# Modulation chunks spread 3, 2, 2, 2, 3, 2, 2, 0 beside the eight gate pairs instead of two beside each

## The chip, the cores and the metric

The kernel runs on one core of a Trainium2 chip. The metric is the time of one execution on the device in microseconds (us). The names of the engines are those of the profile: PE is TensorE (PEld its weight loads), DVE is VectorE, ACT is ScalarE, POOL is GpSimd, and SP issues DMA transfers.

## The reference, cut to what matters

One layer of a hybrid encoder works on 1056 tokens (1024 of a prompt, 32 of a sample) with a model width of 1024. What bears on the change is this:

```python
mod = (jax.nn.silu(c) @ w_ada + b_ada).reshape(B, 6, 1, D_MODEL)
shift1, scale1, gate1, shift2, scale2, gate2 = [mod[:, i] for i in range(6)]
h = _rms_norm(x, norm1_g) * (1 + scale1) + shift1
proj = h @ w_in
q, k, v, xin, gb, gc, ga_br, gb_br = jnp.split(proj, IN_SPLITS, axis=-1)
...
m = jax.nn.sigmoid(ga_br) * y_a + jax.nn.sigmoid(gb_br) * y_b
x = x + gate1 * (m @ w_out)
h2 = _rms_norm(x, norm2_g) * (1 + scale2) + shift2
```

The modulation `mod` is a product of two vectors (one for the prompt, one for the sample) with a 1024 x 6144 matrix. Its parts shift1 and scale1 are needed first of all; gate1, scale2, shift2 and gate2 only behind the attention. Everything is float32.

## The kernel before, in words

Each float32 operand is split into a high and a low part (`split`: an ACT cast, L84, and a subtraction, L85, on DVE as a rule), and a product is three matmuls. The projections of the convolution and of the gates are computed transposed, two blocks of 128 columns at a time, by Strassen's scheme with seven products (`strassen`, L166 to L199): k = 0 to 6 are seven groups of 2 x 12 matmuls (L181), each half of the group 264 columns wide. Behind k = 0 ACT copies a product (L185), behind k = 1 and 2 DVE adds (L188, L191), behind k = 4, 5 and 6 DVE adds the results (L197), and ACT takes the sigmoids (L553); SP stores the gates (L555). `wstrassen` loads (L107) and prepares the weights of a pair.

The stage of the change is the loop over the two gate sections and four pairs of blocks each (L541 to L561): eight gate pairs. Behind the matmuls of each pair stand calls of `ada_step`. Such a step opens one chunk of the modulation and closes an older one. A chunk is 128 of the 6144 columns. To open it (`ada_dve`, L345 to L370) SP loads 512 KB of w_ada (L351, two buffers `adw`), and DVE forms the products along the 1024 rows in an accumulator `adacc`, of which there are also two buffers: 2 instructions L354 and 14 L357, 16 in all. To close it, PE transposes the accumulator's two halves into a PSUM tile `pad` (L364), DVE sums them (L366), adds the bias (L367) and for the section of scale2 forms the gain (L377). A step closes the oldest chunk when more than one is open, and behind the loop the last one is closed (L562). The chunks of this stage are called c0 to c15 here, in the order in which they are opened; chunk c(n) uses the accumulator buffer of c(n-2).

Behind the loop the normalised input is loaded again, block by block, as operand `hA` of the attention's projections (`load_split`, L203 to L207: a DMA L204, a cast L84, a subtraction L85) through a stage tile `st` with two buffers, and then its last 32 columns as `hS` (L577). The first four units of these projections (L731, L732, L733; 24 matmuls each) are issued together, block by block of hA, so 96 matmuls follow hA as it comes. Each unit has a PSUM bank; a fifth unit takes the bank that the first gives back when ACT has read it (L843, L848, L853, L856, the copy of V last). Before these reads a cast of another weight, `wf` (L1033), stands on ACT, whose load (L107) goes through the same stage tile behind hS.

PE's instructions stand in the order in which the code issues them. The instructions of DVE, ACT, POOL and SP are put in order by the framework's scheduler.

Of the kernel before, what the change touches and what calls it, by code (L numbers as in the profile page):

```python
# [38 lines left out]
def hybrid_layer(tc, x_prompt, x_sample, cache_k, cache_v, state_conv, c_prompt, c_sample,  # L39
# [96 lines left out]
    def wstrassen(srcs):  # L136

        raw = [kt_stage(src) for src in srcs]
        A11, A12, A21, A22 = raw[0][:, :4], raw[0][:, 4:], raw[1][:, :4], raw[1][:, 4:]
        w = {}  # L140

        def parts(o, src, eng=None):
            w[o] = ws_tile()
            split(src, w[o][:, 0], w[o][:, 1], eng)

        parts("A11", A11)
        dve.tensor_sub(A11, A11, A21)
        S3 = A11
        dve.tensor_add(A21, A21, A22)
        S1 = A21  # L150
        parts("A22", A22)
        dve.tensor_sub(A22, A22, S3)
        S2 = A22
        parts("S2", S2)
        parts("S1", S1)
        parts("A12", A12)
        dve.tensor_sub(A12, A12, S2)
        S4 = A12
        parts("S3", S3)
        parts("S4", S4, pool)  # L160
        return w
# [4 lines left out]
    def strassen(w, gs, dest, epi, hook=None):  # L166


        st = {g: {} for g in gs}
        for k, (wo_, to_, dst) in enumerate(SEQ):  # L170
            for g in gs:
                q = st[g]
                first = dst not in q
                if first:
                    q[dst] = u_tile()[:, :QW]
                t = Top[to_, g]
                for j in range(4):
                    wh, wl = w[wo_][:, 0, j, :], w[wo_][:, 1, j, :]
                    for n, (l, r) in enumerate(((wh, 0), (wh, 1), (wl, 0))):

                        pe.matmul(q[dst], l, t[:, r, j, :], start=first and j == n == 0, stop=j == 3 and n == 2,  # L181
                                  skip_group_check=not first)
                if k == 0:
                    q["p1"] = tmp("p1")
                    act.copy(q["p1"], q["X"])  # L185
                elif k == 1:
                    q["u2"] = tmp("u2")
                    dve.tensor_add(q["u2"], q["Y"], q["p1"])  # L188
                elif k == 2:
                    q["w"] = tmp("w")  # L190
                    dve.tensor_add(q["w"], q["Z"], q["u2"])  # L191
                elif k == 3:
                    epi(0, 0, g, q["X"])
                else:
                    i, j, other = ((1, 1, "w"), (0, 1, "u2"), (1, 0, "u2"))[k - 4]
                    d = dest(i, j, g)
                    dve.tensor_add(d, q[dst], q[other])  # L197
                    epi(i, j, g, d)
                if hook:  # L199
                    hook(k, g)  # L200
# [8 lines left out]
    def win_pair(sec, n):  # L209
        return [win_v[:, :, (sec * KT + n + i) * P:(sec * KT + n + i + 1) * P] for i in range(2)]  # L210
# [136 lines left out]
    def ada_dve(sec, n, psp, tag, sbp):  # L347

        c = sec * KT + n
        st = sbp.tile([P, KT, P], F32, tag="adw", name="adw", bufs=2)  # L350
        sp.dma_start(st, wada_v[:, :, c * P:(c + 1) * P])  # L351
        acc = sbp.tile([P, 2, P], F32, tag="adacc", name="adacc", bufs=2)
        for s_ in range(2):
            dve.tensor_scalar(out=acc[:, s_, :], in0=st[:, 0, :], scalar1=sc[:, 8 * s_:8 * s_ + 1], scalar2=None,  # L354
                              op0=ALU.mult)
            for kt in range(1, KT):
                dve.scalar_tensor_tensor(out=acc[:, s_, :], in0=st[:, kt, :],  # L357
                                         scalar=sc[:, 8 * s_ + kt:8 * s_ + kt + 1], in1=acc[:, s_, :],
                                         op0=ALU.mult, op1=ALU.add)

        def close():
            pt = psp.tile([P, 512], F32, tag=tag, name="pad", bufs=2)
            for s_ in range(2):
                pe.transpose(pt[:, s_ * P:(s_ + 1) * P], acc[:, s_, :], ident)  # L364
            red = sbp.tile([P, 2], F32, tag="adred", name="adred", bufs=2)
            dve.tensor_reduce(out=red, in_=pt[:, :2 * P].rearrange("p (a b) -> p a b", a=2), axis=AX.X, op=ALU.add)  # L366
            dve.tensor_scalar(out=mod[:, c, :], in0=red, scalar1=vec[:, R_B + c:R_B + c + 1],  # L367
                              scalar2=None, op0=ALU.add)
            if sec == 4:
                scale_gain(a2, 4, n, R_G2)  # L370
        return close
# [80 lines left out]
    def pair_tile():  # L452
        return E.tile([P, 2, T], F32, tag="sg", name="sg", bufs=1)
# [64 lines left out]
    def load_qkv(h):  # L518
        w = q_tiles(h)
        for j in range(3):  # L520
            v = kt_stage(qkv_src(h, j))
            for r in (0, 1):
                split(v[:, 4 * r:4 * r + 4], w[r][0][:, j], w[r][1][:, j])
        return w
# [4 lines left out]
    def ada_step():  # L529
        if ada_todo:  # L530
            ada_open.append(ada_dve(*ada_todo.pop(0), PSB, "x", B))
        if len(ada_open) > 1 or (ada_open and not ada_todo):
            ada_open.pop(0)()
# [9 lines left out]
    for sec, dst in ((6, ga_d), (7, gb_d)):  # L543
        for p in range(0, KT, 2):
            w = wstrassen(win_pair(sec, p))
            sg = pair_tile()

            def dest(i, j, g):
                return sg[:, i, (g + 2 * j) * QW:(g + 2 * j + 1) * QW]

            def epi(i, j, g, src):
                d = dest(i, j, g)
                act.activation(d, src, AF.Sigmoid)  # L553
                if g == 1 and (i, j) in ((0, 1), (1, 0)):
                    sp.dma_start(dst[p + i], sg[:, i])  # L555

            if (sec, p) == (7, KT - 2):
                qkv_w.append(load_qkv(0))
            strassen(w, (0, 1), dest, epi)
            ada_step()  # L560
            ada_step()  # L561
    while ada_open:  # L562
        ada_open.pop(0)()
    B.release()
# [964 lines left out]
```

## Time and profile before

| | before |
|---|---|
| time of the runs shown (3) | 2136.35 us median, 2134.64 to 2137.19 |
| the profiled execution | 2132.99 us, span 2131.2 us |
| mean granted clock of TensorE | 0.982 |
| PE busy | 2031.0 us (95% of the span) |
| DVE busy | 1351.4 us (63%) |
| ACT busy | 847.1 us (40%) |
| gate pair 1 starts on PE at | 245.7 us |
| gate pair 8 ends on PE at | 413.9 us |

The profiled execution is 3.4 us shorter than the median of the runs. Times in a timeline are counted from the start of the span; in a row a first number is a start, a second the duration of the group, and what stands in brackets at the end is how long the engine was idle before it and what ended that. The granted clock (PEclk) is a share of full speed: 1.00 is 2.4 GHz, 0.50 is 1.2 GHz.

### The profile page before, as it was taken

How to read it: one execution, taken by the hardware profiler on the slowest of the kernel's cores; microseconds unless marked ns; L12 is line 12 of the kernel's file. 1: busy time of each engine (PE TensorE's matmuls, PEld its weight loads, DVE VectorE, ACT ScalarE, POOL GpSimd, SP SyncE). 2: the span in 40 equal slices, each digit the busy share in tenths (PEclk: the TensorE clock that was granted, in tenths of full speed). 3: DMA queues.
4: the chain of work that ended last, by engine and by line, in shares of the span. 5: the costliest groups of instructions: out<-in, count | busy, mean ns of one | idle time of the engine just before them, and what ended most of it. 6: DMA issues, size and time to landing. Idle time of an engine off the chain costs nothing. (4 is left out here: it accounts for less than half of the span.)

```text
span 2131.2 us, 37806 instructions
## 1 busy us (share of the span) xinstructions
PE 2031.0 (95%) x14339; PEld 1976.7 (93%) x14339; DVE 1351.4 (63%) x3096; ACT 847.1 (40%) x2044; POOL 364.7 (17%) x660
## 2 busy tenths in 40 slices
PE   7799999899999999999899989889999999999999
PEld 5799999899999999999899989879999999989998
DVE  4988799967766776677357974685555555432322
ACT  5522233366666666666222213463332332321210
POOL 1023100033333333333000000012112112100000
PEclk8899999999999999999999999999999999999999
DMA  8422254532211221121388625123222222552321
GB/s 251 151 84 90 71 161 135 192 89 60 68 57 56 62 59 54 50 69 48 114 258 250 198 90 170 53 68 122 71 73 89 70 80 79 172 157 65 99 69 57
DMA packets 298960, 224.42 MB, mean 105 GB/s; under 512 B 15617, under 2 KB 281498, under 8 KB 298778
## 3 DMA queue, kind: packets, MB, share of 16 engines
q1 hardware_dynamic: 298778, 222.00, 34.0%
q8 instruction: 113, 1.85, 0.4%
q14 instruction: 69, 0.57, 0.1%
HBM read 162.46 MB, written 59.49 MB: 104 GB/s over the span
## 5 line engine op out<-in xcount | busy, mean ns | idle before, releaser
L84 ACT CAST ws<-st 128x512 fp32r<-128x512 f32 x360 | 217.2, 615 | 564.4 <-PE u L181 172.9
L181 PE MATMUL u<-op,ws 128*128 128x264 f32 x3168 | 397.3, 285 | 7.8 <-ACT op L84 6.5
L181 PEld LDWEIGHTS u<-op,ws 128*128 128x128 f32 x3168 | 392.4, 189 | 8.4 <-ACT op L84 6.7
L85 DVE TENSOR_TENSOR ws<-st,ws 128x512 fp32r<-128x512 f32 (+1 forms) x322 | 222.6, 699 | 195.3 <-ACT ws L84 192.9
L181 PE MATMUL u<-T,ws 128*128 128x264 f32 x1536 | 198.5, 287 | 1.2 <-DVE sg L197 1.2
L181 PEld LDWEIGHTS u<-T,ws 128*128 128x128 f32 x1536 | 193.5, 190 | 1.8 <-DVE sg L197 1.8
L731 PE MATMUL b<-qw,hA 128*128 128x384 f32 x512 | 186.8, 365 | 2.5 <-DVE adred L366 1.2
L732 PE MATMUL b<-qw,hA 128*128 128x384 f32 x512 | 174.2, 340 | 0.6 <-DVE qw L688 0.6
L733 PE MATMUL b<-qw,hA 128*128 128x384 f32 x512 | 173.8, 339 | 0.0
L1431 PE MATMUL u<-ka,ws 128*128 128x352 f32 x480 | 156.8, 327 | 4.6 <-ACT ka L84 2.8
L1432 PE MATMUL u<-ka,ws 128*128 128x352 f32 x480 | 155.6, 324 | 2.3 <-DVE ka L85 2.3
L181 PE MATMUL u<-B,ws 128*128 128x264 f32 x1152 | 152.1, 287 | 4.6 <-ACT B L84 4.6
L1433 PE MATMUL u<-ka,ws 128*128 128x352 f32 x480 | 155.7, 324 | 0.0
L181 PEld LDWEIGHTS u<-B,ws 128*128 128x128 f32 x1152 | 145.6, 190 | 5.3 <-ACT B L84 4.9
L357 DVE SCALAR_TENSOR_TENSOR adacc<-adw,sc,adacc 128x128 f32<-128x128 f32 x448 | 132.8, 350 | 0.6
L879 ACT ACTIVATE p<-S,nmx,rs 128x128 f32<-128x128 f32 (+5 forms) x144 | 113.1, 787 | 50.1 <-DVE nmx L959 17.0
L85 POOL TENSOR_TENSOR ws<-st,ws 128x512 fp32r<-128x512 f32 x38 | 49.8, 1311 | 445.3 <-ACT ws L84 426.1
L731 PEld LDWEIGHTS b<-qw,hA 128*128 128x128 f32 x512 | 97.7, 191 | 6.4 <-issue 2.1
L732 PEld LDWEIGHTS b<-qw,hA 128*128 128x128 f32 x512 | 97.9, 191 | 1.2 <-DVE qw L688 0.9
L733 PEld LDWEIGHTS b<-qw,hA 128*128 128x128 f32 x512 | 97.2, 190 | 0.0
L1431 PEld LDWEIGHTS u<-ka,ws 128*128 128x128 f32 x480 | 90.6, 189 | 5.6 <-ACT ka L84 3.5
L1432 PEld LDWEIGHTS u<-ka,ws 128*128 128x128 f32 x480 | 90.7, 189 | 3.1 <-DVE ka L85 3.1
(277 smaller groups left out, 4379.8 us busy)
## 6 DMA issues: line engine op xcount, KB each, us to landing
adw<-in_w_ada_dram SPq DMA_DIRECT2D x48, 512.0 KB, 4.0
st<-in_w_gate_up_dram SPq DMA_DIRECT2D x44, 512.0 KB, 4.0
st<-in_w_in_dram SPq DMA_DIRECT2D x43, 512.0 KB, 4.3
sa<-a_d SPq DMA_DIRECT2D x22, 528.0 KB, 3.6
a_d<-xa SPq DMA_DIRECT2D x84, 132.0 KB, 1.7
st<-in_w_in_dram SPq DMA_DIRECT2D x42, 256.0 KB, 2.9
st<-in_w_down_dram SPq DMA_DIRECT2D x16, 512.0 KB, 5.0
h_d<-xnT SPq DMA_DIRECT2D x8, 528.0 KB, 4.3
```

What stands on the lines that cost most here:

```text
L84: act.copy(hi, src)
L85: (lo_eng or dve).tensor_sub(lo, src, f(hi))
L181: pe.matmul(q[dst], l, t[:, r, j, :], start=first and j == n == 0, stop=j == 3 and n == 2, skip_group_check=not first)
L357: dve.scalar_tensor_tensor(out=acc[:, s_, :], in0=st[:, kt, :], scalar=sc[:, 8 * s_ + kt:8 * s_ + kt + 1], in1=acc[:, s_, :], op0=ALU.mult ...
L731: pe.matmul(pj[:, 0:384], a, qh[:, :, c, :], start=kt == 0, stop=False)
L732: pe.matmul(pj[:, 0:384], a, ql[:, :, c, :], start=False, stop=False)
L733: pe.matmul(pj[:, 0:384], b, qh[:, :, c, :], start=False, stop=kt == KT - 1)
L879: act.activation(p[:n, :u["L"]], u["sv"][m][:n], AF.Exp, bias=u["nmx"][:n, m:m + 1], scale=u["rs_t"][:n, m:m + 1], accum_out=sums[:n, m:m ...
L1431: pe.matmul(pt[:, :gw], wh, ah, start=kt == 0, stop=False)
L1432: pe.matmul(pt[:, :gw], wh, al, start=False, stop=False)
L1433: pe.matmul(pt[:, :gw], wl, ah, start=False, stop=kt == KC - 1)
```

## The change

The two calls behind each gate pair become a number that depends on the pair: 3, 2, 2, 2 behind the four pairs of the first section, and 3, 2, 2, 0 behind those of the second. There are 16 steps in both kernels.

```diff
             strassen(w, (0, 1), dest, epi)
-            ada_step()
-            ada_step()
+            for _ in range((3, 2, 2, (2, 0)[sec == 7])[p // 2]):
+                ada_step()
```

The closings move with the steps. Before, pair 1 closes c0, pairs 2 to 7 two chunks each, and behind pair 8 three are closed: c13, c14 and c15. Now pair 1 closes c0 and c1, pair 5 closes c8, c9 and c10, the other pairs from 2 to 7 two each, and behind pair 8 there is c15 alone.

First place: PE at the end of gate pair 5, from its last product (k = 6) to the first product of pair 6. What each instruction waits for stands in brackets. Before:

```order
L181 MATMUL u_4064<-T41_390,ws_3912 128x264 [waits DVE_49]
L181 MATMUL u_4064<-T41_390,ws_3912 128x264 x11
L364 MATMUL pad_4156<-ident_83,adacc_3880 128x128 [waits PE_49]
L364 MATMUL pad_4156<-ident_83,adacc_3880 128x128
L364 MATMUL pad_4181<-ident_83,adacc_4139 128x128 [waits PE_49]
L364 MATMUL pad_4181<-ident_83,adacc_4139 128x128
L181 MATMUL u_4218<-B110_377,ws_4192 128x264 [waits Activation_49]
```

and now:

```order
L181 MATMUL u_4089<-T41_390,ws_3937 128x264 [waits DVE_49]
L181 MATMUL u_4089<-T41_390,ws_3937 128x264 x11
L364 MATMUL pad_4181<-ident_83,adacc_3905 128x128 [waits PE_49]
L364 MATMUL pad_4181<-ident_83,adacc_3905 128x128
L364 MATMUL pad_4207<-ident_83,adacc_4164 128x128 [waits PE_49]
L364 MATMUL pad_4207<-ident_83,adacc_4164 128x128
L364 MATMUL pad_4233<-ident_83,adacc_4190 128x128 [waits DVE_49,PE_49]
L364 MATMUL pad_4233<-ident_83,adacc_4190 128x128 [waits DVE_49]
L181 MATMUL u_4270<-B110_377,ws_4244 128x264 [waits Activation_49]
```

A third chunk, c10 (adacc_4190), is closed between the two pairs, and its two transposes wait for DVE.

Second place: DVE at the same place, from the last addition of pair 5 on, in the changed kernel. adacc_4190 is c10, adacc_4216 is c11, adred_4184 and adred_4210 are the sums of c8 and c9.

```order
L197 TENSOR_TENSOR sg_3957<-u_4089,u2_4016 128x264 [waits PE_49]
L366 TENSOR_REDUCE adred_4184<-pad_4181 128x2 [waits PE_49]
L354 TENSOR_SCALAR adacc_4190<-adw_4188,sc_106 128x128 [waits DMAHW0_49]
L367 TENSOR_SCALAR mod_114<-adred_4184,vec_105 128x2 [waits DVE_49]
L357 SCALAR_TENSOR_TENSOR adacc_4190<-adw_4188,sc_106,adacc_4190 128x128 [waits DVE_49]
L377 TENSOR_SCALAR a2_119<-mod_114,vec_105 128x2 [waits DVE_49]
L357 SCALAR_TENSOR_TENSOR adacc_4190<-adw_4188,sc_106,adacc_4190 128x128 [waits DVE_49]
L354 TENSOR_SCALAR adacc_4190<-adw_4188,sc_106 128x128
L357 SCALAR_TENSOR_TENSOR adacc_4190<-adw_4188,sc_106,adacc_4190 128x128 [waits DVE_49] x10
L366 TENSOR_REDUCE adred_4210<-pad_4207 128x2 [waits PE_49]
L357 SCALAR_TENSOR_TENSOR adacc_4190<-adw_4188,sc_106,adacc_4190 128x128 [waits DVE_49]
...
```

All 16 instructions of c10 stand behind the sum of c8 (adred_4184), which is what frees their accumulator buffer, and so behind the end of pair 5. Before, c9 stood at this place and was closed a pair later.

Third place: PE behind the last gate pair. Before:

```order
L181 MATMUL u_4943<-T41_390,ws_4769 128x264 x11
L364 MATMUL pad_5035<-ident_83,adacc_4736 128x128 [waits PE_49]
L364 MATMUL pad_5035<-ident_83,adacc_4736 128x128
L364 MATMUL pad_5061<-ident_83,adacc_5018 128x128 [waits PE_49]
L364 MATMUL pad_5061<-ident_83,adacc_5018 128x128 [waits DVE_49]
L364 MATMUL pad_5068<-ident_83,adacc_5044 128x128 [waits DVE_49,PE_49]
L364 MATMUL pad_5068<-ident_83,adacc_5044 128x128 [waits DVE_49]
L731 MATMUL b_5142<-qw_4790,hA_5078 128x384 [waits DVE_49,Activation_49]
```

and now:

```order
L181 MATMUL u_4995<-T41_390,ws_4821 128x264 x11
L364 MATMUL pad_5068<-ident_83,adacc_4788 128x128 [waits PE_49]
L364 MATMUL pad_5068<-ident_83,adacc_4788 128x128
L731 MATMUL b_5142<-qw_4842,hA_5078 128x384 [waits DVE_49,Activation_49]
```

Four transposes and their waits for DVE have gone from here; only c15, which DVE computes beside pair 8, is closed.

## Rows read from the trace of the kernel before

**Rows 1.** The page: busy time of the engines (share of the span, instructions), and the chain of work that ended last, by engine.

```profile
PE 2031.0 (95%) x14339; PEld 1976.7 (93%) x14339; DVE 1351.4 (63%) x3096; ACT 847.1 (40%) x2044; POOL 364.7 (17%) x660
...
PE 30%; DMA 2%; DVE 1%; ACT 1%; issue 0%; POOL 0%; DVEq 0%; ACTq 0%
```

**Rows 2.** Busy time by stretch: gate pairs 2, 5, 6 and 8 and the stretch behind pair 8. The columns are the stretch in us, its length, the busy time (and instructions) of PE, PEld, DVE, ACT and POOL, the granted clock, the DMA share and GB/s. The last row is the DVE line L357 alone beside pair 6, with the same last three columns.

```profile
267.00:288.00 21.00, 21.00 (x175) 21.00 (x174) 16.98 (x41) 8.88 (x22) 1.36 (x1) 1.00 0.52 163
...
330.00:351.00 21.00, 21.00 (x175) 21.00 (x174) 19.96 (x57) 7.71 (x18) 1.29 (x1) 1.00 0.50 153
351.00:372.00 21.00, 21.00 (x175) 21.00 (x174) 20.09 (x58) 7.72 (x18) 1.29 (x1) 1.00 0.48 151
...
393.00:414.00 21.00, 21.00 (x172) 20.82 (x171) 18.82 (x54) 8.57 (x17) 1.35 (x1) 1.00 0.67 215
414.00:425.00 11.00, 1.60 (x8) 0.84 (x7) 9.78 (x30) 4.29 (x6) 0.00 (x0) 0.65 0.62 216
...
351.00:372.00 21.00, 8.01 (x28) 1.00 0.48 151
```

**Rows 3.** The timeline of PE at the end of pair 5 and behind pair 8: start, duration, engine, line, operation.

```profile
350.67 0.60 PE L364 MATMUL pad<-ident,adacc 128*128 128x128 f32 x4
351.02 3.18 PE L181 MATMUL u<-B,ws 128*128 128x264 f32 x24
...
413.91 0.60 PE L364 MATMUL pad<-ident,adacc 128*128 128x128 f32 x4
421.94 0.44 PE L364 MATMUL pad<-ident,adacc 128*128 128x128 f32 x1 [7.44 <-DVE adacc L357]
423.10 0.48 PE L364 MATMUL pad<-ident,adacc 128*128 128x128 f32 x1 [0.71 <-DVE adacc L357]
424.83 0.66 PE L731 MATMUL b<-qw,hA 128*128 128x384 f32 x1 [1.25 <-DVE adred L366]
```

**Rows 4.** The timeline of DVE: the sum of the first chunk closed behind pair 5; the same sum behind pair 6 and the last instruction of the chunk that follows it; the first and the last instruction of c15 behind pair 8.

```profile
351.21 0.41 DVE L366 TENSOR_REDUCE adred<-pad 128x2 f32<-128x256 f32 x1
...
372.21 0.41 DVE L366 TENSOR_REDUCE adred<-pad 128x2 f32<-128x256 f32 x1
378.11 0.35 DVE L357 SCALAR_TENSOR_TENSOR adacc<-adw,sc,adacc 128x128 f32<-128x128 f32 x1
...
418.18 0.28 DVE L354 TENSOR_SCALAR adacc<-adw,sc 128x128 f32<-128x128 f32 x1
...
422.70 0.35 DVE L357 SCALAR_TENSOR_TENSOR adacc<-adw,sc,adacc 128x128 f32<-128x128 f32 x1
```

**Rows 5.** PE alone by stretch, around idle times of several lengths: stretch, length, busy time and matmuls, granted clock, DMA share, GB/s.

```profile
417.40:424.80 7.40, 0.92 (x2) 0.50 0.58 219
424.80:430.80 6.00, 5.97 (x19) 0.50 0.85 255
431.00:436.00 5.00, 5.00 (x30) 1.00 0.56 149
778.50:780.90 2.40, 0.00 (x0) 1.00 0.28 78
781.00:785.00 4.00, 4.00 (x25) 1.00 0.45 129
850.40:853.00 2.60, 0.00 (x0) 1.00 0.90 253
854.40:857.40 3.00, 3.00 (x12) 0.50 0.12 34
1271.20:1273.80 2.60, 2.60 (x10) 0.50 0.00 0
```

**Rows 6.** The timeline of ACT: the casts of the first, the fourth and the eighth block of hA, the cast of wf, and the last read of the first unit's bank.

```profile
407.97 1.08 ACT L84 CAST hA<-st 128x1056 fp32r<-128x1056 f32 x1
...
418.40 1.07 ACT L84 CAST hA<-st 128x1056 fp32r<-128x1056 f32 x1 [1.78 <-DMA st<-h_d]
...
434.17 1.08 ACT L84 CAST hA<-st 128x1056 fp32r<-128x1056 f32 x1 [1.77 <-DMA st<-h_d]
...
441.95 1.05 ACT L1033 CAST wf<-st 128x1024 fp32r<-128x1024 f32 x1 [5.38 <-DMA st<-in_w_in_dram]
...
443.80 0.30 ACT L856 COPY V<-b 128x128 f32<-128x128 f32 x1
```

**Rows 7.** The timeline of DVE: the subtractions of the first, third, fourth and eighth block of hA.

```profile
410.67 1.26 DVE L85 TENSOR_TENSOR hA<-st,hA 128x1056 fp32r<-128x1056 f32 x1
...
416.33 1.26 DVE L85 TENSOR_TENSOR hA<-st,hA 128x1056 fp32r<-128x1056 f32 x1 [1.22 <-ACT hA L84]
...
423.09 1.26 DVE L85 TENSOR_TENSOR hA<-st,hA 128x1056 fp32r<-128x1056 f32 x1
...
435.27 1.26 DVE L85 TENSOR_TENSOR hA<-st,hA 128x1056 fp32r<-128x1056 f32 x1 [1.59 <-ACT hA L84]
```

**Rows 8.** The timeline of SP's queue: the load of c15's columns, the next one (the last weights of the attention's first head), the last store of a gate, and the load of wf.

```profile
399.47 0.38 SPq L351 DMA_DIRECT2D adw<-in_w_ada_dram  x1
400.81 0.37 SPq L107 DMA_DIRECT2D st<-in_w_in_dram  x1
...
419.82 0.32 SPq L555 DMA_DIRECT2D gb_d<-sg  x1
...
436.56 0.38 SPq L107 DMA_DIRECT2D st<-in_w_in_dram  x1
```

## The prediction

> **What bounds the kernel now.** I read the page's busy times and its chain first, then the busy time by stretch from gate pair 5 on, then the timelines of PE and DVE at the ends of pairs 5 and 8, and last those of ACT and SP behind the loop. PE is busy for 95% of the span, and it heads the chain that ended last [rows 1]. So only PE's own wait and its clock count. Beside the gate pairs PE has no idle time at all: 21.00 of 21.00 us at a granted clock of 1.00, DVE beside it at 20 [rows 2]. Behind pair 8 it is the other way round: in 11 us PE has 1.60 us of work and DVE 9.78 [rows 2]. There PE's transposes wait 7.44 and 0.71 us for the accumulators and its first projection 1.25 us for the last sum [rows 3]. The 16 instructions of c15 run from 418.18 to 423.05, after everything that PE had to do [rows 4].
>
> The terms are changes of the profiled execution, 2132.99 us. The median of the runs shown is 3.36 us above it; I add their sum to the median, 2136.35.
>
> **Term 1: a new wait at the end of pair 5.** Behind pair 5 three chunks are closed now. The third, c10, needs the accumulator buffer of c8, which comes free with the sum of c8 (L366), and that needs transposes which stand at the end of the same pair. So all 16 instructions of c10 lie between pair 5 and pair 6, with nothing on PE beside them, and the matmuls of pair 6 stand behind c10's transposes. What this takes is seen behind pair 6 of before: the same work (two sums, their small additions and 16 instructions of a chunk) runs from the sum at 372.21 to 378.11 + 0.35 = 378.46, or 6.25 us [rows 4]. Behind pair 5 the sum starts at 351.21 [rows 4], so c10 is ready at about 357.46. Its second transpose adds 0.2 to 0.3 (four in 0.60 [rows 3]), and pair 6 begins near 357.7 instead of 351.02 [rows 3]: +6.7. The low end, 6.0, is the case that the subtractions of bias and gain are put behind c10; the high end, 7.3, that the scheduler's neighbours (an addition of 0.4, a weight's subtraction) get between. The load of c10's columns is hidden: its buffer is freed in the middle of pair 5.
>
> The third step of pair 1 costs nothing: c0 and c1 have been computed long before, and their four transposes take the 0.60 us that four take anywhere [rows 3]; two of them came at another place before. In pair 2 DVE gets one more chunk's instructions than it had, some 4 us (28 of L357 take 8.01 us for two chunks [rows 2]); it was busy for 16.98 of the pair's 21 us [rows 2], so this fills its slack without passing it. If that cover were gone, the price would be the delay of one addition before k = 6, under 1 us.
>
> **Term 2: the clock behind that wait.** After an idle time of 2.4 us at 778.5 the next matmuls run at 1.00, after one of 2.6 us or more at 850.4 at 0.50 [rows 5]. Behind pair 8 the clock is already at 0.50 during the wait, and the first 19 matmuls take 5.97 us where 30 then take 5.00 [rows 5]: at full speed these 19 would take 3.17, so 2.8 are lost. The wait of 6 us here is more like that one. The smaller losses: 3.00 us at 0.50 at 854.4, which is 1.5 lost, and 2.60 at 1271.2, which is 1.3 [rows 5]. Bounds 0 (the clock stays, as at 778.5) and 3; I take +2.2, between the two long cases.
>
> **Term 3: what the end of the loop gives back.** Behind pair 8 only c15 is closed, and DVE computes it beside that pair, where it had 18.82 us of work in 21 [rows 2] and now has one chunk where two were begun. PE's transposes go at 413.91. Their sum stands on DVE behind the last additions and one subtraction of hA, 1.26 us [rows 7], so the projections begin near 416.5 (415.6 to 417.4) instead of 424.83: 8.3 us earlier. That is not the gain. The 96 matmuls follow hA, whose blocks come through two stage buffers, and the fifth unit waits for ACT to read the first unit's bank. In before that chain ends with the subtraction of the eighth block at 435.27, the load of wf that takes its stage at 436.56, the cast at 441.95, and the copy of V at 443.80 + 0.30 = 444.1 [rows 6, 7, 8]. PE's 96 matmuls end there too: 19 by 430.8, then 77 at 0.167 to 0.175 us [rows 5]. Both ends meet, so the chain's move is what counts.
>
> It moves by less than 8.3. The fourth block's cast ended at 418.40 + 1.07 = 419.47, and DVE, busy with c15, subtracted at 423.09: 3.6 us that go [rows 6, 7]. The first block's subtraction started 1.6 us behind its cast (409.05 to 410.67) because of c14 [rows 6, 7], and c15's 512 KB at 399.47 stood next to the attention's weights at 400.81 on SP [rows 8]. The bounds are 3.6 (only the first of these) and 6.3 (all three, the load at 1.1, a little under the 1.34 us by which it stands ahead of the weights); I take 4.6, since the third and fourth block also follow the gates' additions, and SP's next loads of hA stand behind the stores of gates, which do not move. Term 3: -4.6.
>
> **Term 4: the clock at the end of the 96 matmuls.** Started at 416.5, and without the long wait at full speed, they end about 2.1 us (12 matmuls) behind the eighth block, at 431.9 + 2.1 = 434.0. The bank comes at 444.1 - 4.6 = 439.5. So PE idles there for 5.5 us, which it did not do before, and goes on at 0.50 for a while: +1.9, by the same bounds as term 2 (0 and 3.0).
>
> The half clock of before behind pair 8 costs nothing more in this sum, since the chain, not PE, sets the end there.
>
> **The sum.** +6.7 + 2.2 - 4.6 + 1.9 = +6.2 us: 2139.2 for the profiled execution, 2142.5 on the median.
>
> **A rule that bears on term 1.** PE's row at 424.83 waits for DVE itself [rows 3], so the trace does not show a ready matmul standing behind a waiting transpose. The Trainium skill ("TensorE: Matmul & The Clock Gate", section "Step-by-step: what each phase is for") says that matmuls stay in program order and only weight loads are pulled ahead. By that rule pair 6 cannot pass c10's transposes, and the sum is +6.2; if it could, terms 1 and 2 would fall away, and -2.7 would be left. No run here shows it yet.
>
> **The rivals.**
>
> A. Faster or equal, by one mechanism: behind the loop DVE's backlog alone, not the chain over wf, holds the 96 matmuls. Then they end at about 433.2, the bank is free when PE wants it, and term 3 is -10.9 with no term 4: +6.7 + 2.2 - 10.9 = -2.0, so 2134.3. For it speaks that the wait named in the rows is DVE's; against it, that wf's cast stood 5.38 us behind its DMA [rows 6] and its load needs the stage of the last blocks. It decides if wf is cast before 434.
>
> B. The new wait does not come: c10 is computed early, or pair 6 passes the transposes. -4.6 + 1.9 = -2.7, so 2133.6. Against it stands the order of DVE, where c10 follows the sum of c8.
>
> C. DVE falls behind in pair 6 as well: it has 20.09 us of work in 21 [rows 2], and c11 and c12 follow c10 closely. If PE's late start did not give DVE the time back, up to 3.9 us more (one chunk, by half of the 8.01 us [rows 2]) would be waited for at pair 6's end: 2146.4. Against it: c10, which before ran beside pair 6, has been done before it begins.
>
> **Chances.** The forecast 0.75, A 0.10, B 0.07, C 0.08. With all terms at their low ends the forecast gives 6.0 - 6.3 = -0.3, with all at their high ends 7.3 + 3.0 - 3.6 + 3.0 = +9.7, so its own range is 2136.0 to 2146.1. The range 2135.0 to 2147.0 adds a us on either side for the scatter of the runs, takes in C, and leaves out A, B and little else, under 2 in 10. About 0.2%, or 4.3 us, is what a measurement of this kernel can tell from no change. Of the forecast's 0.75 some 0.13 lies below +4.3; A and B lie mostly within 4.3 of the median, and perhaps a third of them beyond it. So slower 0.69, same 0.25, faster 0.06.
>
> **What would show it.** Term 1: in the changed kernel PE's transposes at about 351 carry a wait of 5 to 6 us for adacc, and pair 6 begins 6.7 us after pair 5's end. Term 2: a stretch at 0.50 behind it. Term 3: the wait behind pair 8 falls below 3 us, and the eighth block of hA is subtracted 4.6 us nearer to the end of pair 8. Term 4: PE idles before the fifth unit, ACT casts wf in that time, and the clock is 0.50 afterwards. The prediction is wrong if pair 6 begins within 2 us of pair 5's end, if PE's wait moves to another pair, or if the fifth unit begins without a gap.

## The result and the profile after

| | before | changed |
|---|---|---|
| median of 8 runs | 2135.02 us (2133.54 to 2137.19) | 2142.59 us (2138.14 to 2145.33) |
| ratio to before, 95% interval | | 1.003 (1.0021 to 1.0039) |
| profiled execution, span | 2132.99, 2131.2 us | 2142.27, 2140.5 us |
| mean granted clock | 0.982 | 0.982 |

The change made the kernel slower by 0.3%, which is 6.4 us by the ratio (4.5 to 8.3). The forecast was 2142.5 us. The page alone says little: PE has 5 us more of busy time, and DVE and ACT have the same.

```profile
PE 2036.2 (95%) x14339; PEld 1981.8 (93%) x14339; DVE 1351.9 (63%) x3096; ACT 846.4 (40%) x2044; POOL 364.5 (17%) x660
```

The rows that answer to [rows 3] are in PE's timeline of the changed kernel: the end of pair 5, then what follows pair 8.

```profile
350.54 0.60 PE L364 MATMUL pad<-ident,adacc 128*128 128x128 f32 x4
356.26 0.45 PE L364 MATMUL pad<-ident,adacc 128*128 128x128 f32 x1 [5.12 <-DVE adacc L357]
357.42 0.47 PE L364 MATMUL pad<-ident,adacc 128*128 128x128 f32 x1 [0.71 <-DVE adacc L357]
357.55 5.58 PE L181 MATMUL u<-B,ws 128*128 128x264 f32 x24
...
422.58 0.38 PE L364 MATMUL pad<-ident,adacc 128*128 128x128 f32 x2
425.35 0.41 PE L731 MATMUL b<-qw,hA 128*128 128x384 f32 x1 [2.39 <-DVE adred L366]
...
448.71 0.69 PE L731 MATMUL b<-qw,hA 128*128 128x384 f32 x1 [4.23 <-ACT V L856]
...
463.22 0.44 PE L731 MATMUL b<-qw,hA 128*128 128x384 f32 x1 [0.34 <-ACT o L892]
```

Three things are to be seen. At pair 5's end PE now waits 5.12 and 0.71 us for c10. The first 24 matmuls of pair 6 then take 5.58 us where 24 took 3.18 in [rows 3]. Behind pair 8 the wait of 7.44 us has become 2.39, and a new one of 4.23 us stands before the fifth projection unit. The last row is a matmul in the attention that has the same short wait in every profile; it serves as a mark below.

Busy time by stretch (the columns of [rows 2]) of the changed kernel shows who works while PE waits, and the clock:

```profile
351.20:356.20 5.00, 0.00 (x0) 0.00 (x0) 5.00 (x17) 0.48 (x2) 1.26 (x1) 0.99 1.02 345
357.60:362.90 5.30, 5.30 (x25) 5.30 (x25) 5.30 (x23) 0.38 (x1) 0.00 (x0) 0.50 0.37 105
363.00:372.00 9.00, 9.00 (x75) 9.00 (x75) 7.62 (x22) 1.95 (x5) 0.00 (x0) 1.00 0.30 86
```

DVE is busy for all of the 5.00 us in which PE does nothing, ACT and POOL for only 0.48 and 1.26: DVE computes c10, and only then can PE transpose it. Behind the wait the clock is 0.50 for 5.30 us, then 1.00 again. DVE's timeline gives the length, as [rows 4] did for pair 6 of before: the sum of c8, and the last instruction of c10.

```profile
351.09 0.41 DVE L366 TENSOR_REDUCE adred<-pad 128x2 f32<-128x256 f32 x1
...
357.03 0.34 DVE L357 SCALAR_TENSOR_TENSOR adacc<-adw,sc,adacc 128x128 f32<-128x128 f32 x1
```

That is 357.37 - 351.09 = 6.28 us; the prediction had 6.25. And the rows of the loop's end that answer to [rows 6 to 8]: the eighth block of hA (its load, cast and subtraction), the load and the cast of wf, and the copy of V. They come from the timelines of SP, ACT and DVE.

```profile
434.80 0.32 SPq L204 DMA_DIRECT2D st<-h_d  x1
...
442.44 0.38 SPq L107 DMA_DIRECT2D st<-in_w_in_dram  x1
```

```profile
440.05 1.07 ACT L84 CAST hA<-st 128x1056 fp32r<-128x1056 f32 x1 [3.46 <-DMA st<-h_d]
...
446.74 1.04 ACT L1033 CAST wf<-st 128x1024 fp32r<-128x1024 f32 x1 [5.31 <-DMA st<-in_w_in_dram]
...
448.37 0.29 ACT L856 COPY V<-b 128x128 f32<-128x128 f32 x1
```

```profile
441.15 1.26 DVE L85 TENSOR_TENSOR hA<-st,hA 128x1056 fp32r<-128x1056 f32 x1 [3.27 <-ACT hA L84]
```

Times in a span also carry what happened earlier in that execution, so all comparisons below are of stretches. From the transposes at pair 5's end to the mark, before has 458.44 - 350.67 = 107.77 us (the matching row of before's PE timeline is the first of the next fence), the changed kernel 463.22 - 350.54 = 112.68: +4.9. The profiled times differ by 9.3. The other 4.4 us stand behind the mark, where the two programs do the same work; a second profile of each was taken for that reason.

```profile
458.44 0.45 PE L731 MATMUL b<-qw,hA 128*128 128x384 f32 x1 [0.34 <-ACT o L892]
```

### The profile page after: what moved, and what is told of

Same layout as the page of the kernel before. It is cut to its first block, busy times and chain, and to the rows that moved or that the text cites. A ratio compares the mean times of both kernels' runs of the same rounds, so it can differ in the third digit from the quotient of the medians.

```text
span 2140.5 us, 37805 instructions
## 1 busy us (share of the span) xinstructions
PE 2036.2 (95%) x14339; PEld 1981.8 (93%) x14339; DVE 1351.9 (63%) x3096; ACT 846.4 (40%) x2044; POOL 364.5 (17%) x660
## 5 line engine op out<-in xcount | busy, mean ns | idle before, releaser
L357 DVE SCALAR_TENSOR_TENSOR adacc<-adw,sc,adacc 128x128 f32<-128x128 f32 x448 | 132.8, 349 | 0.5
```

## The experiments

The theory: the wait for c10 and the half clock behind it cost 8.8 us, the end of the loop gives some 4 back. Every kernel of this section but the two repetitions was run 9 to 12 times, beside runs of the kernel before. In this section and its expectations the end of pair 8 is the end of its last product. The table at the section's end puts their stretches beside their times.

**The changed kernel and the one before once more.** No edit.

> The changed kernel once more, for a second profile. If the 4.5 us that the first profile lost behind the fifth unit belong to the change, they stand there again; if they are the clock's scatter between runs, the stretch from 470 us to the end differs from before's by another amount, anywhere from -3 to +5 us, while the wait at pair 5 (5.1 and 0.7 us) and the slow matmuls behind it repeat within 0.5 us.

> The kernel before once more, for a second profile. If the scatter is the clock's, the stretch from 470 us to the end differs by up to 4 us between the two profiles of one kernel; the waits behind pair 8 (7.4, 0.7 and 1.3 us) repeat within 0.5 us. If it does not differ by over 1 us, the 4.5 us belong to the change.

The changed kernel took 2139.01 us, with the same waits to the hundredth at pair 5. The matmuls behind them take 5.12 us, where they took 5.58:

```profile
348.38 0.60 PE L364 MATMUL pad<-ident,adacc 128*128 128x128 f32 x4
354.10 0.45 PE L364 MATMUL pad<-ident,adacc 128*128 128x128 f32 x1 [5.12 <-DVE adacc L357]
355.26 0.48 PE L364 MATMUL pad<-ident,adacc 128*128 128x128 f32 x1 [0.71 <-DVE adacc L357]
355.38 5.12 PE L181 MATMUL u<-B,ws 128*128 128x264 f32 x24
...
419.96 0.38 PE L364 MATMUL pad<-ident,adacc 128*128 128x128 f32 x2
...
445.88 0.69 PE L731 MATMUL b<-qw,hA 128*128 128x384 f32 x1 [4.11 <-ACT V L856]
461.56 0.45 PE L731 MATMUL b<-qw,hA 128*128 128x384 f32 x1 [0.34 <-ACT o L892]
```

Its stretch to the mark is 461.56 - 348.38 = 113.18. Before, again, took 2134.69 us. Here are its PE rows, and ACT's at the loop's end:

```profile
351.37 0.60 PE L364 MATMUL pad<-ident,adacc 128*128 128x128 f32 x4
...
458.59 0.45 PE L731 MATMUL b<-qw,hA 128*128 128x384 f32 x1 [0.34 <-ACT o L892]
```

```profile
443.88 0.39 ACT L843 ACTIVATE sq<-b 128x256 f32<-128x256 f32 x1 [1.27 <-PE b L733]
...
444.57 0.30 ACT L856 COPY V<-b 128x128 f32<-128x128 f32 x1
```

Its stretch is 107.22, so the two profiles of one kernel agree within 0.6 us there. Behind the mark (span less the mark's start) before has 1672.8 and 1674.3 us, the changed kernel 1677.3 and 1675.6. Between the second profiles the difference is 1.3 us, not 4.5. The kernels below have 1668.8 to 1678.9 there, and the one with before's own steps 1675.9. So before's first profile was a lucky one behind the mark, and what the first comparison lost there is, for the most part, scatter between executions. The means of the two profiles, 1673.5 and 1676.5, differ by some 3 us; that a part of this belongs to the change is not excluded by these runs.

**Third closing moved from pair 5 to pair 8.**

```diff
-for _ in range((3, 2, 2, (2, 0)[sec == 7])[p // 2]):
+for _ in range((3 - (sec == 7), 2, 2, 2 - (sec == 7))[p // 2]):
```

> The steps stand as 3, 2, 2, 2, 2, 2, 2, 1: the third step of pair 5 goes to pair 8, where it opens c15 and closes c14. My theory (the third closing of pair 5 costs a wait and a half clock of 8.8 us, and the end of the loop gives 4.1 back): no wait at any pair's end, the fifth projection unit 3.0 to 4.1 us earlier than in the kernel before, 2131 to 2132.5 us, ratio to before 0.998 to 0.9985. Rival (the end of the loop gives nothing of its own, the gain only looks like one because PE comes late): as before, ratio 0.9995 to 1.0005. Rival (any other distribution of steps costs something later in the kernel, 4.5 us of the profiled difference stood there): slower than before, ratio 1.000 to 1.002.

Measured: 2132.31 us against 2135.81, ratio 0.9976 (0.9967 to 0.9985): faster than before.

```profile
351.49 0.60 PE L364 MATMUL pad<-ident,adacc 128*128 128x128 f32 x4
351.84 3.18 PE L181 MATMUL u<-B,ws 128*128 128x264 f32 x24
...
418.54 0.41 PE L731 MATMUL b<-qw,hA 128*128 128x384 f32 x1 [3.45 <-DVE mod L367]
439.10 0.45 PE L731 MATMUL b<-qw,hA 128*128 128x384 f32 x1 [3.49 <-ACT V L856]
...
453.62 0.44 PE L731 MATMUL b<-qw,hA 128*128 128x384 f32 x1 [0.34 <-ACT o L892]
```

There is no wait at pair 5, and the loop's end keeps its gain. The third step of pair 1, which this kernel and the changed one have, shows no cost: from the first product of pair 1 to pair 5's transposes they take 104.99 and 104.79 us, before 104.97. Both rivals fall: the loop's end gives something of its own, and another distribution than before's does not cost something later. The gain is larger than expected, 5.9 us to the fifth unit, with an interval that just reaches 0.9985: the eighth block of hA was cast 3.6 us behind the issue of its load, in the changed kernel 5.2.

**Third step at pair 5 alone.** The counterpart: 2, 2, 2, 2, 3, 2, 2, 1.

```diff
-for _ in range((3, 2, 2, (2, 0)[sec == 7])[p // 2]):
+for _ in range((2 + (sec == 7), 2, 2, 2 - (sec == 7))[p // 2]):
```

> Steps 2, 2, 2, 2, 3, 2, 2, 1: the third step at pair 5 alone, none at pair 1. My theory: the third chunk closed behind pair 5 is c9 now, whose buffer is c7's, closed at the same place; so the wait is there as in the changed kernel (5 to 6 us and a half clock, 8.6 to 9.0 us), and the end of the loop gives 4 to 6 back: ratio 1.001 to 1.0025. Rival (the wait came from the chunk ahead that the third step of pair 1 makes): no wait at pair 5, ratio as with 3, 2, 2, 2, 2, 2, 2, 1.

Measured: 2140.80 against 2138.75, ratio 1.0014 (1.0002 to 1.0027). The wait is there without the step of pair 1, for c9 this time, so the rival falls:

```profile
355.76 0.45 PE L364 MATMUL pad<-ident,adacc 128*128 128x128 f32 x1 [5.26 <-DVE adacc L357]
356.52 0.47 PE L364 MATMUL pad<-ident,adacc 128*128 128x128 f32 x1 [0.32 <-DVE adacc L357]
356.65 4.29 PE L181 MATMUL u<-B,ws 128*128 128x264 f32 x24
```

Pair 6 begins 6.4 us later behind pair 5's transposes than in before, and its first 24 matmuls lose 1.1 us. Together that is 7.5 us, less than the 8.6 to 9.0 expected; the ratio is inside its range.

**A third accumulator.** The changed kernel with three buffers.

```diff
-acc = sbp.tile([P, 2, P], F32, tag="adacc", name="adacc", bufs=2)
+acc = sbp.tile([P, 2, P], F32, tag="adacc", name="adacc", bufs=3)
```

> The changed kernel with a third accumulator buffer, so that c10 no longer needs c8's. My theory (it is the buffer, and so the place of the 16 instructions of c10 behind the end of pair 5): no wait of PE at 351, pair 6 begins within 0.5 us of pair 5's transposes, ratio to before 0.998 to 0.999. Rival (three closings at one place cost by themselves, by their transposes, sums and PSUM tiles): a wait of 1 us or more stays, ratio above 1.000.

Measured: 2133.96 against 2135.81, ratio 0.9991 (0.998 to 1.0002).

```profile
351.35 0.60 PE L364 MATMUL pad<-ident,adacc 128*128 128x128 f32 x4
352.37 0.44 PE L364 MATMUL pad<-ident,adacc 128*128 128x128 f32 x2 [0.42 <-DVE adred L366]
352.56 0.61 PE L181 MATMUL u<-B,ws 128*128 128x264 f32 x3
```

The same three closings cost a wait of 0.42 us, for a sum and no longer for an accumulator (the third tile `pad` has the place of the first; there are two). Pair 6 begins 1.21 us behind pair 5's transposes, later than the 0.5 expected and far from the 7.0 of the changed kernel. So it was the buffer, not their number. The ratio lies just above the theory's range, and its interval takes in the rival's 1.000 too; it is the wait that decides. The loop's end gave less here than with the step moved to pair 8, and why is left open.

**PE kept busy while it waits.** The changed kernel, with transposes of the identity into c10's tile ahead of c10's own.

```diff
+            if tag == "x" and (sec, n) == (4, 2):
+                for _ in range(54):
+                    pe.transpose(pt[:, 0:P], ident, ident)
```

> The changed kernel, in which PE makes 54 transposes of the identity into c10's tile while it waits for c10 (their results are overwritten). My theory: the wait's length stays (pair 6 begins 6.0 to 7.0 us behind pair 5's transposes), the clock stays at 1.00, and the first 24 matmuls of pair 6 take 3.1 us, not 5.6: 2.3 us faster than the changed kernel, ratio to before 1.002 or a little under. Rival (the half clock in pair 6 costs nothing at the end, since what follows has slack): same time as the changed kernel, ratio 1.003.

Measured: 2140.10 against 2135.81, ratio 1.0015 (1.0005 to 1.0025). PE's timeline, and a stretch of pair 6 (the columns of [rows 2]):

```profile
353.67 0.60 PE L367 MATMUL pad<-ident,adacc 128*128 128x128 f32 x4
354.69 6.11 PE L365 MATMUL pad<-ident 128*128 128x128 f32 x54 [0.42 <-DVE adred L369]
...
360.78 3.19 PE L181 MATMUL u<-B,ws 128*128 128x264 f32 x24
```

```profile
360.90:364.00 3.10, 3.10 (x28) 3.10 (x27) 3.10 (x13) 0.38 (x1) 0.00 (x0) 1.00 0.64 174
```

Pair 6 comes as late as in the changed kernel (360.78 - 353.67 = 7.1 us behind pair 5's transposes, there 357.55 - 350.54 = 7.0), but at 1.00 its 24 matmuls take 3.19 us and not 5.58. So the half clock came with PE's idle time. It costs 2.4 us there and 1.9 in the second profile, and to the mark this kernel is 1.8 to 2.3 us faster (+3.4 in the table below, against +5.2 and +5.7). By the whole times alone the two could not be told apart for certain: their intervals overlap a little.

**c10 closed inside pair 6.** The third step of pair 5 is issued behind k = 2 of pair 6.

```diff
-            strassen(w, (0, 1), dest, epi)
+            strassen(w, (0, 1), dest, epi,
+                     (lambda k, g: ada_step() if (k, g) == (2, 1) else None) if (sec, p) == (7, 2) else None)
-            for _ in range((3, 2, 2, (2, 0)[sec == 7])[p // 2]):
+            for _ in range((3 - (sec == 7), 2, 2, (2, 0)[sec == 7])[p // 2]):
```

> The third step of pair 5 is issued behind the third product (k = 2) of pair 6, some 9 us later. My theory: c10 is ready by then, so no wait at the end of pair 5 and none at the new place. But DVE has c10, c11 and c12 in pair 6, 12 us beside 12 of other work in 21, so a wait of 0.5 to 4 us at the end of pair 6 (rival C of the prediction): the fifth unit is 0 to 4 us earlier than before, ratio 0.998 to 1.000. Rival (the clock or the delay comes from elsewhere in pair 6): ratio 1.002 or more, as in the changed kernel.

Measured: 2138.28 against 2135.81, ratio 1.0013 (1.0005 to 1.0022). Pair 6 starts without a wait, and inside pair 7, which begins at 374.78, there is one:

```profile
353.21 0.60 PE L364 MATMUL pad<-ident,adacc 128*128 128x128 f32 x4
353.56 3.18 PE L181 MATMUL u<-B,ws 128*128 128x264 f32 x24
...
381.25 7.40 PE L181 MATMUL u<-T,ws 128*128 128x264 f32 x46 [3.04 <-DVE ws L85]
```

The wait is not for an accumulator: DVE, with a third chunk's work in one pair, has put off the subtractions of pair 7's weights. It is busy for 20.99 of the 21.20 us of pair 6 and for all of the time from there to the end of PE's wait. This is the overload of rival C, 3.04 us and a stretch at half clock behind it. In the changed kernel it doesn't come up: PE has no wait at the ends of pairs 6 and 7, and c10 has been done before pair 6 begins.

**The first cast of wf behind ACT's reads of the first unit, in the changed kernel and with 3, 2, 2, 2, 2, 2, 2, 1.**

```diff
         act.copy(vdst, src()[:n, 256:384])
+        if k == 0:
+            wh, wl, wv = late.pop()
+            act.copy(wh, wv)
+            dve.tensor_sub(wl, wv, f(wh))
...
-            act.copy(wh, v)
+            if n:
+                act.copy(wh, v)
+            else:
+                late.append((wh, wl, v))
...
```

> The changed kernel with the first cast of wf (and its subtraction) behind ACT's reads of the first projection unit, not ahead of them; nothing else moves. My theory of the loop's end (chain over the stage, wf and ACT): PE's idle 4.2 us before the fifth unit goes, the fifth unit begins 21 to 22.5 us behind the end of pair 8 instead of 26.0, and the kernel is 3.5 to 4.5 us faster than the changed one: ratio to before 1.0005 to 1.0015. Rival A of the prediction (DVE's backlog alone held the 96 matmuls, wf is not last): the fifth unit where it was, ratio 1.003.

> Steps 3, 2, 2, 2, 2, 2, 2, 1 and the first cast of wf behind the reads of the first unit. By the theory the gains add: the fifth unit 20.5 to 22 us behind the end of pair 8 (24.5 with the steps alone, 30.4 before), 3 us faster than the steps alone: 2128 to 2130 us, ratio to before 0.9955 to 0.997. Rival (what is gained at the loop's end is given back where the attention waits for wf or for the next head's weights, which share its stage): as with the steps alone, ratio 0.9975.

Measured: 2141.34 against 2136.86, ratio 1.002 (1.001 to 1.003), and 2132.26, ratio 0.9974 (0.9964 to 0.9984). In the changed kernel PE's 4.23 us before the fifth unit go (it begins 19.8 us behind the end of pair 8), which refutes rival A; wf is cast at 446.74 in the changed kernel, too, and not before 434. But a little later PE waits again, because the cast, whose load has not landed, now holds up the reads of the second unit:

```profile
449.30 0.44 PE L756 MATMUL b<-ident,qd 128*128 128x128 f32 x2 [2.94 <-ACT V L856]
```

To the mark, 2.6 to 3.1 of the expected 3.5 to 4.5 us are gained. In the whole time the interval overlaps that of the changed kernel. With the moved steps the fifth unit comes at 22.2 us, and the 3 us over the steps alone are not there: 1.4 by the stretch, none by the times.

**The cast behind the reads of the fourth unit, with 3, 2, 2, 2, 2, 2, 2, 1 and with the steps of before.** The same edit with `k == 3`.

> Steps 3, 2, 2, 2, 2, 2, 2, 1, and the first cast of wf behind ACT's reads of the fourth projection unit (behind the first unit's reads it stood ahead of the second's, and PE waited 0.5 to 3 us there). My theory: PE has no wait over 1 us from its first projection to the seventh unit, the point 465 us of before is reached 7.5 to 9 us earlier than in before, and the ratio is 0.996 to 0.997. Rival (the gain is used up by the scatter of the later stages or by wf arriving late for its own matmuls): as with the steps alone, 0.9975.

> The kernel before (steps 2 and 2) with the same later cast of wf and nothing else. If both ends met at 444 us in before, as the prediction had it (the chain over wf and PE's 96 matmuls), the fifth unit begins where it did, 30 us behind the end of pair 8, and the ratio is 0.9995 to 1.0005. If the chain over wf alone held it, the fifth unit comes earlier by 1 us or more.

Measured: 2132.15 against 2138.75, ratio 0.997 (0.9959 to 0.9982), and 2137.55, ratio 0.9997 (0.9987 to 1.0008). With the steps of before nothing that the times could show is gained. The fifth unit came 29.2 us behind the end of pair 8, in before 30.4. By the letter of the expectation that is its second reading, but the 1.2 us are not wf's: fewer of the 96 matmuls ran at half clock, 9 and not 18, which start 0.32 us apart where the others start 0.175 apart, and this is 1.3 us (PE's stretch with the columns of [rows 5], where 424.8 to 430.8 has 0.50).

```profile
424.30:427.10 2.80, 2.80 (x9) 0.50 0.74 216
```

In before PE's matmuls, not wf, were last, which is the first of the two readings but for the clock. With the other steps only a wait of 1.49 us is left before the mark (1 was expected at most), which is reached 7.3 us earlier (7.5 to 9 were expected, for a point a little later). This is the fastest by its stretch; from the kernel with the moved steps alone the times can't tell it.

| kernel | pair 5's transposes to the mark, us | less before's mean of 107.5 | whole time, by the ratio (95%) |
|---|---|---|---|
| before, two profiles | 107.8, 107.2 | | |
| changed, two profiles | 112.7, 113.2 | +5.2, +5.7 | +6.4 (4.5 to 8.3) |
| 3, 2, 2, 2, 2, 2, 2, 1 | 102.1 | -5.4 | -5.1 (-7.0 to -3.2) |
| 2, 2, 2, 2, 3, 2, 2, 1 | 110.5 | +3.0 | +3.0 (0.4 to 5.8) |
| changed, three accumulators | 105.5 | -2.0 | -1.9 (-4.3 to 0.4) |
| changed, PE kept busy | 110.9 | +3.4 | +3.2 (1.1 to 5.3) |
| changed, c10 closed in pair 6 | 110.7 | +3.2 | +2.8 (1.1 to 4.7) |
| changed, wf behind unit 1 | 110.0 | +2.6 | +4.3 (2.1 to 6.4) |
| 3, 2, 2, 2, 2, 2, 2, 1, wf behind unit 1 | 100.7 | -6.8 | -5.6 (-7.7 to -3.4) |
| the same, wf behind unit 4 | 100.2 | -7.3 | -6.4 (-8.8 to -3.8) |
| before, wf behind unit 4 | 107.0 | -0.5 | -0.6 (-2.8 to 1.7) |

The whole time's column is (ratio - 1) times the median of before in the same comparison. In every row the stretch of 108 us accounts for the difference within its interval. What the changes did happened there and nowhere else that these runs can tell.

## Why the prediction was right

**Term 1 (+6.7).** Pair 6 begins 357.55 - 350.54 = 7.01 us behind pair 5's transposes, in before 0.35: +6.66. Its cause was the buffer, as the third accumulator and the step at pair 5 alone show. Rival B, no new wait, is out. The rule of the Trainium skill ("TensorE: Matmul & The Clock Gate", section "Step-by-step: what each phase is for"), that matmuls keep their order, agrees with the trace: pair 6's matmuls, which had all they needed at this place in before, start right behind c10's second transpose, at 357.55; in the 5 us ahead only DVE, with c10, had much to do.

**Term 2 (+2.2).** 5.58 - 3.18 = 2.4 us in the first profile and 5.12 - 3.18 = 1.9 in the second, behind the same waits; and in the kernel in which PE was kept busy, with all else as it was, the same matmuls took 3.19.

**Term 3 (-4.6).** From pair 8's last transposes to the copy of V, 448.37 - 422.58 = 25.8 us against 443.80 - 413.91 = 29.9: -4.1, and -4.3 between the second profiles (25.6 and 29.8). The size holds; how it was put together does not. The step "the chain's move is what counts" took the chain over wf to end with PE in before. But PE has no idle time between its first projection and the fifth unit in either profile of before. In the first the two ends do meet (the copy of V is done at 444.10, the fifth unit begins at 444.49); in the second ACT waits 1.27 us for PE, and moving wf away from before gained nothing that the times show. So PE was last there, and the chain had 0.4 us to spare in the one and over 1.27 in the other; only in the changed kernel is the chain last. And the chain moved by less than 4.6: the eighth block's load was issued 4.1 us earlier, counted from pair 8's transposes (434.80 - 422.58 against 430.19 - 413.91), but its cast began 5.2 us behind that instead of 4.0. This is the row of SP's queue in before, to which 434.80 answers:

```profile
430.19 0.33 SPq L204 DMA_DIRECT2D st<-h_d  x1
```

The block's subtraction is 2.8 us nearer to pair 8's end, not 4.6. Most of the rest of the -4.1, 1.1 us, comes from the load of wf, whose time the prediction took as unchanged: its cast begins 4.30 us behind the issue (446.74 - 442.44), in before 5.39 (441.95 - 436.56). Why the block's load took longer in the changed kernel, and wf's less, stays open.

**Term 4 (+1.9).** PE's wait was forecast at 5.5 us and is 4.23. From the copy of V to the mark the changed kernel takes 463.22 - 448.37 = 14.85 us, before 458.44 - 443.80 = 14.64: +0.2. Between the second profiles it is 461.56 - 445.54 = 16.02 against 458.59 - 444.57 = 14.02: +2.0. So the term was over-sized in one pair and met in the other, within its bounds of 0 and 3.0. How long the half clock lasted was not the same: from the fifth unit to the mark the granted clock is 0.90 and 0.81 in the two profiles of the changed kernel, and 1.00 in both of before.

```profile
445.54 0.29 ACT L856 COPY V<-b 128x128 f32<-128x128 f32 x1
```

**The sum (+6.2)** is +4.9 and +6.0 in the profiles (first with first, second with second), and +6.4 in the times. That the median came out within 0.1 us of 2142.5 is luck: single terms are off by up to 1.7 us, and single executions of the changed kernel lie from 2138 to 2145.

**Rival C** was the right fear at the wrong place. As forecast it doesn't decide in the changed kernel, but when c10 was closed inside pair 6, with its work still there, it came, a pair later and at weights.

## What to carry to other kernels

Where a producer has n buffers and its consumer stands in a fixed order on a busy engine, more than n uses in one place put the producer's whole work for each use beyond n on that engine's path, however idle the producer's buffers look before. Spreading work evenly is not the aim; it is that no place takes back more buffers than exist, and that the last place, where nothing covers the work, takes back only what is computed. Here one number in the table, 1 step moved from pair 5 to the last pair, turned +0.3% into -0.24%.

## What the runs showed of the hardware

The same wait of PE sometimes halves the clock and sometimes doesn't. [Rows 5] have matmuls at 1.00 behind the wait at 778.5 and at 0.50 behind the one at 850.4; in the first profile of the changed kernel it is the other way round at the same two places of the program. PE's timeline and its stretches (the columns of [rows 5]):

```profile
785.75 0.30 PE L821 MATMUL b<-ident,on 128*128 128x128 f32 x1 [2.49 <-DVE K L948]
...
858.93 0.30 PE L821 MATMUL b<-ident,on 128*128 128x128 f32 x1 [2.73 <-DVE K L948]
```

```profile
786.00:789.00 3.00, 3.00 (x13) 0.53 0.41 115
...
859.00:862.00 3.00, 3.00 (x18) 1.00 0.38 110
```

In the second profiles of both kernels the clock is 1.00 behind both waits. So the prediction's reading of these rows, that 2.4 us keep the clock and 2.6 lose it, was too neat: the waits are 2.49 and 2.73 us in all four profiles, and either was followed by either level. With the steps 3, 2, 2, 2, 2, 2, 2, 1 even the 3.45 us ahead of 418.54 kept it:

```profile
418.60:424.00 5.40, 5.40 (x31) 1.00 0.93 322
```

The waits of 5.1 and 0.7 us lost it in each of the three profiles that have them (the changed kernel twice, and with wf behind unit 1). That this chance is part of why executions of one kernel differ by several us is likely but not shown. It is one more reason why a difference of 6 us had to be sought in one stretch of two traces and not in their spans.
